# Decode attention inside a weight-bound stream: the key turns of a half batch moved behind three points of the half before it

## The chip, the cores and the metric

The kernel runs on one core of a Trainium2 chip. The metric is the time of one execution on the device in microseconds. A profile of one execution gives the trace. Engines are named as the profile names them: PE (TensorE, the matrix engine; PEld is its weight loads), DVE (VectorE), ACT (ScalarE), POOL (GpSimd), SP (SyncE, which issues DMAs).

## What is computed

One layer of a hybrid decoder for two groups of tokens with shared weights: a prompt of 512 tokens and a sample group of 8 sequences with 4 new tokens each, whose 4096 past positions lie in a paged cache. The layer is a gated feed-forward block, a mixer (a gated linear recurrence beside latent attention), and a second feed-forward block. The change is in the attention of the sample group over its cache, in the absorbed latent form:

```python
past_c = cache_kv_latent[l][page_table].reshape(Bs, past_len, KV_LORA)   # 256 wide
past_r = cache_k_rope[l][page_table].reshape(Bs, past_len, QK_ROPE)      # 64 wide
...
s = (einsum('bqhr,bsr->bhqs', ql, c_kv) + einsum('bqhd,bsd->bhqs', qr, k_rope)) * scale
s = where(k_pos <= q_pos, s, -inf)
p = softmax(s, axis=-1)
return einsum('bhqs,bsr->bqhr', p, c_kv)
```

Each of the 8 sequences has 16 queries (4 tokens by 4 heads) against 4096 keys.

## The kernel before

The prompt's tokens and the sample's are cut into two column halves, a and b (256 and 288 columns). Weights are fetched in tiles of 128x1024 (`wraw`, on SP's queue) and split into a high part on ACT (`wh`, L253) and a low part on DVE (`wl`, L254); every product takes three matmuls on PE (`wh` by high, `wh` by low, `wl` by high). Almost all of PE's time is this stream.

The decode of the sample group runs inside the second feed-forward block of column half a. Two generators are stepped in turn: `gb`, the feed-forward block (`ffn`), and `ga`, the decode (`decode`), so that the decode's small pieces stand among weight matmuls in program order. The order of each engine's instructions is then fixed when the program is built, by a scheduler that keeps to the program order as far as data allow. Each engine runs its list in order.

The feed-forward steps that are named below, all on column half a: `sil` from the gate's accumulator (DVE L337), three activations `sit` (ACT L323 to L325), the gate product (DVE L339), the product with the up projection (DVE L368), and the split of the result into `hha` (ACT L173) and `hla` (DVE L174). Down projections are copied or added into `ma` (ACT L393, DVE L395).

The decode goes by half batches, class `Half`: half n belongs to sequence n // 2 and holds 2048 of its keys (two gathered blocks `craw`, 128 partitions by 8 rows by 256). There are 16. A half passes these steps:

- `gather` and `gather_r` fetch the latent rows and the rotary rows (`rk`) by indirect DMA on POOL.
- `turn(st)`, four times: the keys of one group of 64 latent columns are turned by two 32x32-block transposes on DVE (`kh`, L1391), one for each block. Four `kh` buffers stand, so one half's turns fit.
- `score`: 64 small matmuls on PE against the four `kh`, in the order of the turns, and 16 against `rk` (L1409), one burst. Two copies bring the scores to `e` (L1411), and DVE takes the row maximum `mxh` (L1413; this instruction is kept as `top`).
- `peak`: PE transposes the maximum (`pm`, L1419), DVE reduces it (L1421) and spreads it with a mask, summed into `mbd` (L1424); ACT takes the exponential (L1425); DVE transposes the probabilities (`pt`, L1427); and 16 small copies place them in `pbuf` (L1431), 12 on ACT and 4 on DVE.
- `value`: 16 matmuls of `pbuf` with `craw` (L1440), the sequence's two halves into one accumulator; after the second half ACT copies it out (L1443) and `gathered` sums it on PE (L1448) and DVE (L1449).

`qsplit(b)` lays out the queries of sequence b in one of two buffers (L1261, two copies on DVE and two on ACT). In `score`, after `top` of a sequence's second half, it is called for the next sequence.

`decode` runs a step count n with five sub-steps, `st` 0 to 4. In step n the turns are those of half n - 2, whose score comes at `st` 4 (`RUN`); the half n - 3 has its `peak` at `st` 1 and its `value` at `st` 4, behind that score. `TURNS` says how many turns are written at each `st`: (2, 1, 1, 0, 0). The first one of a step is tied with `tc.issue_after` behind `top` of half n - 3: the scheduler may not place it earlier.

Of the kernel before, what the change touches and what calls it, by code (L numbers as in the profile page):

```python
# [14 lines left out]
ALU = mybir.AluOpType  # L15
# [6 lines left out]
NB = 8  # L22
# [22 lines left out]
SCALE = 1.0 / float(np.sqrt(192.0))  # L45
# [20 lines left out]
KHB = 4  # L66
STEPS = 5
PEAK, RUN = 1, 4
TURNS = (2, 1, 1, 0, 0)
LEVELS = (32, 16, 8, 4, 2, 1)  # L70
CH = 64

# [41 lines left out]
def hybrid_step_kernel(  # L114
# [5 lines left out]
    nc = tc.nc  # L120
# [12 lines left out]
    def mk(shape, dt, tag, bufs=1, pool=None):  # L133
        return (pool or cur[-1]).tile(shape, dt, name=tag, tag=tag, bufs=bufs)
# [10 lines left out]
    def ps(name, tag="ps", own=False):  # L145
        if tag == "ps" and not own:
            tag = CYC[turns[0] % 4]
            turns[0] += 1
        return pp.tile([P, 512], F32, name=name, tag=tag, bufs=NPS[tag])
# [422 lines left out]
    with scope("ffn0") as pool:  # L572
# [143 lines left out]
        if True:  # L716
            if True:
                sst.close()
                st = stg.enter_context(tc.tile_pool(name="st", bufs=1, side="right", reuse_waits="tile"))
# [73 lines left out]
    with scope("mix") as mx_:  # L793
# [293 lines left out]
        with scope("at2"):  # L1087
# [168 lines left out]
            def qsplit(b):  # L1256
                q = qbd[b % 2]
                bs = slice(b * 16, b * 16 + 16)
                for g in range(4):
                    gs = slice(g * 32, g * 32 + 32)  # L1260
                    (nc.scalar.copy if g % 2 else nc.vector.tensor_copy)(q[gs, :, g % 2 * 16 : g % 2 * 16 + 16], qrep[gs, :, bs])  # L1261
# [49 lines left out]
    with scope("dec"):  # L1311
# [3 lines left out]
        sel4, selL = dq[:, 0, 13 * P : 13 * P + 32], dq[:, 0, 13 * P + 32 : 13 * P + 48]  # L1315
# [45 lines left out]
        class Half:  # L1361
# [32 lines left out]
            def score(self):  # L1394
                q = qbd[self.b % 2]
                self.s = [ps("s", own=True) for _ in range(2)]
                for st, js in enumerate(JS):
                    for jj, j in enumerate(js):
                        for c in range(4):
                            for r in range(2):  # L1400
                                rs = slice(r * 64, r * 64 + 64)
                                as_ = slice(c % 2 * 4, c % 2 * 4 + 4)
                                if j < 8:
                                    kh = self.kh[st][rs, c // 2, as_, jj]
                                    out = self.s[r][c * 32 : c * 32 + 32, :P]
                                else:
                                    kh = self.rk[c // 2][rs, :, jj, as_].rearrange("p i a k -> p a i k")
                                    out = self.s[r][c * 32 : c * 32 + 32, :P].rearrange("p (a i k) -> p a i k", a=4, i=2)
                                nc.tensor.matmul(out, q[rs, j], kh, start=st + jj == 0, stop=st == len(JS) - 1 and jj == 1, skip_group_check=True)  # L1409
                for r in range(2):  # L1410
                    (nc.vector.tensor_copy if r else nc.scalar.copy)(self.e[:, r * P : r * P + P], self.s[r][:, :P])  # L1411
                self.mx = mk([P, 1], F32, "mxh", 2)
                self.top = nc.vector.tensor_reduce(self.mx, self.e, axis=AX.X, op=ALU.max)  # L1413
                if self.i and self.b + 1 < NB:
                    qsplit(self.b + 1)

            def peak(self):
                pm = ps("pm", "pm")[:, :P]
                nc.tensor.matmul(pm, self.mx.broadcast_to([P, P]), ident, start=True, stop=True, skip_group_check=True)  # L1419
                m = m3[:, self.i, self.bs]  # L1420
                nc.vector.tensor_reduce(m, pm.rearrange("p (g q) -> p q g", q=16), axis=AX.X, op=ALU.max)  # L1421
                mq = mk([P, 16], F32, "mq", 2)
                mb = mk([P, 1], F32, "mbd", 2)
                nc.vector.scalar_tensor_tensor(mq, m, -SCALE, selL, op0=ALU.mult, op1=ALU.mult, accum_out=mb)  # L1424
                nc.scalar.activation(self.e, self.e, AF.Exp, scale=SCALE, bias=mb, accum_out=Lc[:, self.i, 0, self.b : self.b + 1])  # L1425
                pt = mk([P, ROWS, 32], F32, "pt", 2)
                nc.vector.transpose(pt.rearrange("p a k -> p (a k)"), self.e)  # L1427
                for c in range(4):
                    for g in range(4):
                        src = pt[c * 32 : c * 32 + 32, g // 2 * 4 : g // 2 * 4 + 4, g % 2 * 16 : g % 2 * 16 + 16]  # L1430
                        (nc.scalar.copy if g else nc.vector.tensor_copy)(self.p[g * 32 : g * 32 + 32, c // 2, c % 2 * 4 : c % 2 * 4 + 4, self.i * 16 : self.i * 16 + 16], src)  # L1431

            def value(self, mate, c):
                i = self.i
# [16 lines left out]
        def decode():  # L1451
            H = [Half(n) for n in range(NH2)]
            blocks = [h_ for h_ in H for _ in range(2)]
            ups = [(h_, st) for h_ in H for st in range(len(JS) - 1)]

            def gather(n=1):
                for h_ in blocks[:n]:
                    h_.gather()
                del blocks[:n]

            def turn(top):
                if ups:
                    h_, st = ups.pop(0)
                    with tc.issue_after(top.ins) if top is not None else nullcontext():
                        h_.turn(st)

            for n in range(NH2 + 4):

                def at(k):
                    return H[n - k] if 0 <= n - k < NH2 else None  # L1470

                for st in range(STEPS):
                    if st == RUN and at(2):
                        at(2).score()
                    if n < 3 and st == 0:
                        gather(2 + n // 2)
                    if st == 0 and 0 <= n - 1 < NH2:
                        at(1).gather_r()
                    if st == PEAK and at(3):
                        at(3).peak()  # L1480
                    if st == 1 and at(4) and at(4).i:
                        at(4).gathered()
                    if st == RUN and at(3):
                        for c in range(2):
                            at(3).value(at(4), c)
                            gather()
                    if n > 1:
                        for i in range(TURNS[st]):
                            turn(at(3).top if at(3) and st + i == 0 else None)
                    yield  # L1490

        def decode_end():
# [33 lines left out]
            nc.vector.tensor_copy(oT[1][:, NH:, HS[1] - TS :], o[:, :P].rearrange("p (h t) -> p h t", h=NH))  # L1526

        ga, gn = decode(), decode_new()
        na, ib = STEPS * (NH2 + 2) + 4, 0
        for ia in range(na):  # L1530
# [191 lines left out]
```

## Time and profile before

| | |
|---|---|
| median of three runs | 1257.47 us (1255.41 to 1258.70) |
| the profiled execution | 1259.31 us |
| its span, first to last instruction | 1257.5 us |
| granted TensorE clock, mean | 0.994 |
| busy ACT / POOL | 59% / 8% |
| decode bursts (L1409), first and last start | 712.1 and 953.0 us |

The page gives busy time by engine, the span in slices, the chain of work that ended last and the costliest groups of instructions. A row of a timeline reads: start in us, duration in us, engine, line, operation, output <- inputs, shape, count, and in brackets the idle time of that engine before it and what ended it. In the list of waits a row gives who waited for what, the total in us, how often, and the longest. A window row gives the busy time of PE, PEld, DVE, ACT and POOL with their counts. A matmul on 32-bit floats stands as two records.

### The profile page before, as it was taken

What the parts mean: (1) busy time and instruction counts of PE and PEld (TensorE: products, weight loads), DVE (VectorE), ACT (ScalarE), POOL (GpSimd) and SP (SyncE); (2) the same over time, 40 slices, a digit from 0 to 9 for tenths busy, and PEclk for the clock granted to TensorE, in tenths of its full rate; (3) what the DMA queues carried; (4) which work ended last, traced back from release to release, by engine and by line L of the source; (5) the groups of instructions that cost most, each with busy time, mean ns of one, the idle gap of its engine ahead of it and who ended that gap; (6) DMA issues with size and microseconds to landing.
All of it is one profiled execution on the core that took longest, in us unless ns stands there. A gap on an engine that the chain in (4) does not pass through costs nothing.

```text
span 1257.5 us, 30075 instructions
## 1 busy us (share of the span) xinstructions
PE 1217.1 (97%) x12366; PEld 1155.1 (92%) x12366; DVE 965.2 (77%) x1945; ACT 739.1 (59%) x1559; POOL 105.2 (8%) x112
## 2 busy tenths in 40 slices
PE   8999999999999999999999999889999999999997
PEld 7999999999999988988888988778787999999997
DVE  7897778878679887877876988787887878466665
ACT  7675545454566654446668765554656777554454
POOL 0000000000000000000002243432530000000000
PEclk9999999999999999999999999999999999999999
DMA  6232323332165121324226769777786635545551
GB/s 235 85 118 94 99 95 101 101 98 84 51 226 166 60 91 58 104 79 145 82 86 242 278 220 322 257 254 279 251 270 218 207 106 191 191 135 182 151 152 59
DMA packets 73914, 195.63 MB, mean 156 GB/s; under 512 B 13136, under 2 KB 28528, under 8 KB 69040
## 3 DMA queue, kind: packets, MB, share of 16 engines
q1 hardware_dynamic: 64800, 150.50, 37.0%
q0 software_dynamic: 7680, 41.95, 9.3%
q8 instruction: 97, 1.59, 0.5%
q10 hardware_dynamic: 1296, 1.26, 0.4%
q14 instruction: 41, 0.34, 0.1%
HBM read 184.00 MB, written 9.67 MB: 154 GB/s over the span
## 4 chain that ended last, share of the span: by engine, by line
PE 85%; ACT 7%; DVE 5%; issue 2%; DMA 0%; SPq 0%; DVEq 0%; another core or an unknown queue 0%; ACTq 0%
PE acc L262 30%; PE acc L280 17%; PE dn L262 8%; PE Y L578 6%; PE X L578 4%; PE Z L578 4%; PE acc L734 3%; PE s L1409 2%; PE o L1440 2%; ACT wh L253 2%; DVE kh L1391 1%; ACT pbuf L1431 1%; PE pa L956 1%; PE s L1206 1%; DVE wl L254 1%
## 5 line engine op out<-in xcount | busy, mean ns | idle before, releaser
L253 ACT CAST wh<-wraw 128x1024 fp32r<-128x1024 f32 (+2 forms) x194 | 184.9, 958 | 180.7 <-PE acc L262 99.3
L254 DVE TENSOR_TENSOR wl<-wraw,wh 128x1024 fp32r<-128x1024 f32 (+2 forms) x194 | 214.8, 1110 | 81.6 <-ACT wh L253 75.7
L280 PE MATMUL acc<-uha,wh 128*128 128x256 f32 (+1 forms) x528 | 155.5, 295 | 0.7 <-issue 0.7
L280 PE MATMUL acc<-ula,wh 128*128 128x256 f32 (+1 forms) x528 | 151.8, 288 | 0.0
L280 PE MATMUL acc<-uha,wl 128*128 128x256 f32 (+1 forms) x528 | 151.3, 287 | 0.3 <-issue 0.2
L262 PE MATMUL acc<-uhb,wh 128*128 128x288 f32 (+1 forms) x432 | 128.0, 296 | 0.0
L262 PE MATMUL acc<-uhb,wl 128*128 128x288 f32 (+1 forms) x432 | 127.0, 295 | 1.0 <-DVE wl L254 0.7
L262 PE MATMUL acc<-ulb,wh 128*128 128x288 f32 (+1 forms) x432 | 127.5, 295 | 0.0
L280 PEld LDWEIGHTS acc<-uha,wh 128*128 128x128 f32 x528 | 100.5, 191 | 8.2 <-issue 7.6
L280 PEld LDWEIGHTS acc<-ula,wh 128*128 128x128 f32 x528 | 100.6, 191 | 1.5 <-issue 1.2
L280 PEld LDWEIGHTS acc<-uha,wl 128*128 128x128 f32 x528 | 100.5, 190 | 1.5 <-issue 0.9
L262 PEld LDWEIGHTS acc<-uhb,wl 128*128 128x128 f32 x432 | 81.2, 188 | 1.6 <-DVE wl L254 1.6
L262 PEld LDWEIGHTS acc<-uhb,wh 128*128 128x128 f32 x432 | 81.0, 187 | 0.2 <-ACT uhb L173 0.2
L262 PEld LDWEIGHTS acc<-ulb,wh 128*128 128x128 f32 x432 | 81.1, 188 | 0.1
L1383 POOL DMA_INDIRECT rk<-pool_r,idr x64 | 67.2, 1051 | 147.5 <-PE s L1409 124.5
L262 PE MATMUL dn<-hh,dh 128*128 128x272 f32 x256 | 74.3, 290 | 0.0
L262 PE MATMUL dn<-hh,dl 128*128 128x272 f32 x256 | 73.7, 288 | 0.0
L262 PE MATMUL dn<-hl,dh 128*128 128x272 f32 x256 | 73.6, 288 | 0.0
L280 PE MATMUL acc<-uhb,wh 128*128 128x272 f32 x176 | 52.8, 300 | 0.0
L262 PE MATMUL acc<-hlb,wh 128*128 128x288 f32 x176 | 52.1, 298 | 0.0
L262 PE MATMUL acc<-hhb,wh 128*128 128x288 f32 x176 | 51.8, 298 | 0.0
L262 PE MATMUL acc<-hhb,wl 128*128 128x288 f32 x176 | 51.4, 294 | 0.0
(634 smaller groups left out, 3875.7 us busy)
## 6 DMA issues: line engine op xcount, KB each, us to landing
wraw<-w_u SPq DMA_DIRECT2D x66, 512.0 KB
wraw<-w_g SPq DMA_DIRECT2D x65, 512.0 KB
wraw<-w_d SPq DMA_DIRECT2D x40, 384.0 KB
wraw<-w_in SPq DMA_DIRECT2D x24, 512.0 KB
wraw<-w_d SPq DMA_DIRECT2D x32, 320.0 KB
wraw<-w_d SPq DMA_DIRECT2D x16, 512.0 KB
wraw<-w_o SPq DMA_DIRECT2D x16, 512.0 KB
g_S<-state SPq DMA_DIRECT2D x4, 512.0 KB
```

The costliest lines, as they stand in the source:

```text
L253: nc.scalar.copy(wh[:, :kt], w[:, :kt])
L254: nc.vector.tensor_tensor(wl[:, :kt], w[:, :kt], f32(wh[:, :kt]), op=ALU.subtract)
L262: nc.tensor.matmul(out, a, b, start=n == 0, stop=n == last)
L280: nc.tensor.matmul(acc[:, :n], a[:, k], b[:, k], start=k + i == 0, stop=k == kt - 1 and i == 2)
L578: nc.tensor.matmul(bank, a[p][:, k], b[q][:, k], start=first and k + n == 0, stop=k == 3 and n == 2, skip_group_check=True)
L734: nc.tensor.matmul(accs[x, d], wts[d][p][:, k], hs[k // 2][q][:, k % 2, x], start=k + n == 0, stop=k == nf - 1 and n == 2)
L956: nc.tensor.matmul(po[es, c].rearrange("p (n m) -> p n m", m=m), kx[:, cs], up(qx[:, cs], m), start=True, stop=True, skip_group_check=True)
L1206: nc.tensor.matmul(s[:, :N], a_, b_, start=n == 0, stop=False, skip_group_check=True)
L1383: nc.gpsimd.indirect_dma_start(rk[:, i].rearrange("p j a k -> p (j a k)"), None, pool_r, off)
L1391: nc.vector.transpose(kh[:, g].rearrange("p a j k -> p a (j k)"), src)
L1409: nc.tensor.matmul(out, q[rs, j], kh, start=st + jj == 0, stop=st == len(JS) - 1 and jj == 1, skip_group_check=True)
L1440: nc.tensor.matmul(o[g : g + 32, :R], self.p[:, c, a], self.craw[c][:, a], start=i + c == 0 and a < 4, stop=i + c == 2 and a >= 4, skip_gr ...
```

## The change

```diff
-TURNS = (2, 1, 1, 0, 0)
+TURNS = (1, 1, 2, 0, 0)
...
                 self.top = nc.vector.tensor_reduce(self.mx, self.e, axis=AX.X, op=ALU.max)
-                if self.i and self.b + 1 < NB:
-                    qsplit(self.b + 1)
...
-                nc.vector.scalar_tensor_tensor(mq, m, -SCALE, selL, op0=ALU.mult, op1=ALU.mult, accum_out=mb)
+                self.spread = nc.vector.scalar_tensor_tensor(mq, m, -SCALE, selL, op0=ALU.mult, op1=ALU.mult, accum_out=mb)
...
-                        (nc.scalar.copy if g else nc.vector.tensor_copy)(self.p[g * 32 : g * 32 + 32, c // 2, c % 2 * 4 : c % 2 * 4 + 4, self.i * 16 : self.i * 16 + 16], src)
+                        put = (nc.scalar.copy if g else nc.vector.tensor_copy)(self.p[g * 32 : g * 32 + 32, c // 2, c % 2 * 4 : c % 2 * 4 + 4, self.i * 16 : self.i * 16 + 16], src)
+                        if g == 0:
+                            self.placed = put
...
+                    if st == 2 and at(2) and at(2).i and at(2).b + 1 < NB:
+                        qsplit(at(2).b + 1)
...
                     if n > 1:
-                        for i in range(TURNS[st]):
-                            turn(at(3).top if at(3) and st + i == 0 else None)
+                        for _ in range(TURNS[st]):
+                            turn(getattr(at(3), ("top", "spread", "placed")[st]) if at(3) else None)
```

Per step one turn is written behind `top` of the half before (the row maximum), one behind `spread` (the masked sum), and two behind `placed` (the last of DVE's four copies into `pbuf`), each tied there. Before, only the first of two turns at `st` 0 was tied, and the others had no tie. The call of `qsplit` moves from the end of `score` to `st` 2 of the step in which the sequence's second half is scored, which is ahead of that score. Nothing else changes; lines from the moved call on shift by two (L1421 becomes L1419, L1431 becomes L1429).

DVE's list from the maximum of half 0 (`mxh`) on, where half 1's turns stand (`kh` from `ha` and `hb`). Before:

```order
L1391 STREAM_TRANSPOSE kh<-hb 128x512
L1421 TENSOR_REDUCE q_8193<-pm 128x16
L337 TENSOR_TENSOR sil<-acc,rna 128x256
L1424 SCALAR_TENSOR_TENSOR mq,mbd<-q_8193 128x16
L1391 STREAM_TRANSPOSE kh<-ha 128x512
L1391 STREAM_TRANSPOSE kh<-hb 128x512
L1427 STREAM_TRANSPOSE pt<-q_8193 128x256
L254 TENSOR_TENSOR wl<-wraw,wh 128x1024
L1431 COPY pbuf<-pt 32x4x16 x4
L339 TENSOR_TENSOR sil<-sil,sit 128x256
L254 TENSOR_TENSOR wl<-wraw,wh 128x1024
L368 TENSOR_TENSOR sil<-sil,acc 128x256
```

The same place after the change, from the spread on:

```order
L1422 SCALAR_TENSOR_TENSOR mq,mbd<-q_8193 128x16
L1391 STREAM_TRANSPOSE kh<-ha 128x512
L1391 STREAM_TRANSPOSE kh<-hb 128x512
L1425 STREAM_TRANSPOSE pt<-q_8193 128x256
L254 TENSOR_TENSOR wl<-wraw,wh 128x1024
L1429 COPY pbuf<-pt 32x4x16 x4
L339 TENSOR_TENSOR sil<-sil,sit 128x256
L1391 STREAM_TRANSPOSE kh<-ha 128x512
L1391 STREAM_TRANSPOSE kh<-hb 128x512
L1391 STREAM_TRANSPOSE kh<-ha 128x512
L1391 STREAM_TRANSPOSE kh<-hb 128x512
L368 TENSOR_TENSOR sil<-sil,acc 128x256
```

The last two turns, four transposes, moved from ahead of the reduction of `pm` to behind the copies into `pbuf`.

DVE's list for half 11 (its keys are in `uhb` and `ha`), before, from the gate's `sil` on:

```order
L337 TENSOR_TENSOR sil<-acc,rna 128x256
L1391 STREAM_TRANSPOSE kh<-ha 128x512
L1391 STREAM_TRANSPOSE kh<-uhb 128x512
L1421 TENSOR_REDUCE q_8193<-pm 128x16
L1449 COPY q_8793<-o 128x4x16
L339 TENSOR_TENSOR sil<-sil,sit 128x256
L1424 SCALAR_TENSOR_TENSOR mq,mbd<-q_8193 128x16
L1391 STREAM_TRANSPOSE kh<-ha 128x512
L368 TENSOR_TENSOR sil<-sil,acc 128x256
L1427 STREAM_TRANSPOSE pt<-q_8193 128x256
L254 TENSOR_TENSOR wl<-wraw,wh 128x1024
L1431 COPY pbuf<-pt 32x4x16 x4
```

After, from the spread on:

```order
L1422 SCALAR_TENSOR_TENSOR mq,mbd<-q_8193 128x16
L1449 COPY q_8793<-o 128x4x16
L1391 STREAM_TRANSPOSE kh<-uhb 128x512
L1425 STREAM_TRANSPOSE pt<-q_8193 128x256
L1391 STREAM_TRANSPOSE kh<-ha 128x512
L1429 COPY pbuf<-pt 32x4x16 x4
L368 TENSOR_TENSOR sil<-sil,acc 128x256
L1391 STREAM_TRANSPOSE kh<-uhb 128x512
L1391 STREAM_TRANSPOSE kh<-ha 128x512
L1391 STREAM_TRANSPOSE kh<-uhb 128x512
L174 TENSOR_TENSOR hla<-sil,hha 128x256
L1391 STREAM_TRANSPOSE kh<-ha 128x512
```

Ahead of the gate's `sil` stood five of the half's transposes before, and stand two after; six now follow the spread, four of them the copies, and `hla` stands before the last one. In halves 2, 5 and 8 the end of the list reads the same way. ACT's list at half 11 is unchanged (exponential, `wh`, twelve copies to `pbuf`, `hha`); at half 2 it is not:

```order
-L1425 ACTIVATE q_8193<-q_8193,mbd 128x256
-L253 CAST wh<-wraw 128x768
-L173 CAST hha<-sil 128x256
-L1431 COPY pbuf<-pt 32x4x16 x12
+L1423 ACTIVATE q_8193<-q_8193,mbd 128x256
+L253 CAST wh<-wraw 128x768
+L1429 COPY pbuf<-pt 32x4x16 x12
+L173 CAST hha<-sil 128x256
```

There `hha`, for which `hla` waits, moved behind the twelve copies. The copies of `qsplit` (L1261) keep their places on both engines. PE's list is the same but for the first burst, whose pieces between weight matmuls are fewer. SP's and POOL's lists are the same.

## The prediction

> **What bounds the kernel now.** I read the page first: the span, the busy shares, the chain that ended last.
>
> ```profile
> span 1257.5 us, 30075 instructions
> ...
> PE 1217.1 (97%) x12366; PEld 1155.1 (92%) x12366; DVE 965.2 (77%) x1945; ACT 739.1 (59%) x1559; POOL 105.2 (8%) x112
> ...
> PE 85%; ACT 7%; DVE 5%; issue 2%; DMA 0%; SPq 0%; DVEq 0%; another core or an unknown queue 0%; ACTq 0%
> ```
>
> TensorE is the bound. Its order of work is the same before and after, but for pieces of the first burst, so the change can only alter what TensorE waits for. Two more views narrow this to the stretch in which half batches 1 to 15 are decoded (half h is batch h//2, part h%2): the busy time by window, and TensorE's waits from 700 to 970.
>
> ```profile
> 728.00:970.00 242.00, 222.35 (x4116) 194.98 (x4115) 192.44 (x434) 141.15 (x383) 85.92 (x85) 0.99 0.76 257
> ...
> PE o L1440 <- issue: 7.9, 5, 2.5
> PE s L1409 <- issue: 4.0, 2, 2.0
> ...
> PE o L1440 <- ACT sit L323: 1.0, 1, 1.0
> ...
> PE o L1440 <- ACT pbuf L1431: 0.9, 1, 0.9
> PE pm L1419 <- DVE mxh L1413: 0.6, 1, 0.6
> ```
>
> TensorE (the first pair) idles 242.0 - 222.35 = 19.7 us there: the most that any edit of the decode order can win. Only the last two waits, 1.5 us, are of the chain that the change shortens. The 11.9 us of "issue" sit in or just behind a score burst, and I read them as code loads: TensorE's instructions arriving late. One is this, in half 8's burst:
>
> ```profile
> 841.84 2.03 PE L1409 MATMUL s<-kh,q 64*32 64x128 f32 x128
> ...
> 846.34 0.41 PE L1409 MATMUL s<-rk,q 64*32 64x128 f32 x3 [2.00 <-issue]
> ...
> q8 instruction: 1, 0.02, 1.0%
> ...
> q8 instruction: 97, 1.59, 0.5%
> ```
>
> The window 841 to 847 holds one packet of the instruction queue (third row). The page has 97 for 2 x 12366 TensorE instructions, 255 each. A burst issues 320 records in 2.5 us, so one packet covers less than a burst. VectorE is 192.44/242 = 80% busy, with little room to catch up.
>
> **The layout of the next batch's queries** (four copies at L1261, ahead of seven batches) is written two steps earlier, but its copies stand in the same places in both built programs, on VectorE and ScalarE. I cost it at 0.
>
> **The turns.** Count and kind are unchanged: eight transposes a half. Two leave for the wait behind `spread`, four go behind `placed`. Before, most of them filled VectorE's gap right after `top`. What they must meet is the burst: it reads turn by turn, and the last transpose is needed after 52 of its 64 key matmuls. Half 11's 128 key records take 892.23 to 894.00, 1.77 us, so that point is start + 1.77 x 52/64 = 1.44 us.
>
> Half 1 can be read off almost directly:
>
> ```profile
> 732.72 1.05 ACT L253 CAST wh<-wraw 128x1024 fp32r<-128x1024 f32 x1 [2.68 <-PE pm L1419]
> ...
> 733.99 0.50 ACT L1425 ACTIVATE q<-q,mbd 128x256 f32<-128x256 f32 x1
> ...
> 734.06 0.67 DVE L1391 STREAM_TRANSPOSE kh<-hb 128x512 f32<-128x512 f32 x1
> 734.65 0.41 DVE L1427 STREAM_TRANSPOSE pt<-q 128x256 f32<-128x256 f32 x1
> 734.98 1.18 DVE L254 TENSOR_TENSOR wl<-wraw,wh 128x1024 fp32r<-128x1024 f32 x1
> 736.09 0.82 DVE L1431 COPY pbuf<-pt 32x64 f32<-32x64 f32 x4
> 736.94 0.42 DVE L339 TENSOR_TENSOR sil<-sil,sit 128x256 f32<-128x256 f32 x1
> ...
> 735.73 2.03 PE L1409 MATMUL s<-kh,q 64*32 64x128 f32 x128
> ```
>
> `pt`, the low weight part, the four copies and the gate product keep their order, and `pt` can't go earlier, since ScalarE's exponential before it (L1425) stands behind a weight cast that starts at 732.72 either way. Behind the gate product now stand four transposes: 737.30 + 4 x 0.61 = 739.75 (the step of two neighbours is 0.59 to 0.63, as 734.06 to 734.65). Needed: 735.73 + 1.44 = 737.17. **Late by 2.55**, where before the last was done at 734.73.
>
> Half 11 adds a second stop:
>
> ```profile
> 884.62 0.42 DVE L1413 TENSOR_REDUCE mxh<-q 128x1 f32<-128x256 f32 x1 [0.46 <-DVE q L1411]
> 884.95 0.70 DVE L1391 STREAM_TRANSPOSE kh<-uhb 128x512 f32<-128x512 f32 x1
> ...
> 888.16 0.42 DVE L337 TENSOR_TENSOR sil<-acc,rna 128x256 f32<-128x256 f32 x1
> ...
> 890.99 0.71 DVE L1391 STREAM_TRANSPOSE kh<-ha 128x512 f32<-128x512 f32 x1
> ...
> 888.16 1.05 ACT L253 CAST wh<-wraw 128x1024 fp32r<-128x1024 f32 x1 [2.53 <-PE acc L280]
> ...
> 891.62 1.04 ACT L253 CAST wh<-wraw 128x1024 fp32r<-128x1024 f32 x1
> 892.68 3.08 ACT L1431 COPY pbuf<-pt 32x64 f32<-32x64 f32 x12
> 895.78 0.41 ACT L173 CAST hha<-sil 128x256 fp32r<-128x256 f32 x1
> ...
> 892.23 2.03 PE L1409 MATMUL s<-kh,q 64*32 64x128 f32 x128
> 894.00 0.74 PE L1409 MATMUL s<-rk,q 64*32 64x128 f32 x32
> ```
>
> After the two transposes of the first turn VectorE now stands before the gate's read (L337), which needs TensorE until 888.16; the other six of the eight transposes, which ran between 886.17 and 891.70 (first and last row above), are no longer in front of `spread`. Then, at the spacing of the rows of before: low part 889.21 to 890.31 (behind the cast), maximum, gate product, spread to 890.95, output copy and one transpose to 891.77, `pt` 891.9, one transpose, four copies to 893.7, `sil` to 894.03, three transposes to 895.84. Now comes `hla` (L174), which needs ScalarE's `hha`, queued behind the twelve `pbuf` copies: 896.15. So `hla` at 896.17, the last transpose 896.53 to 897.2. Needed: 893.67. **Late by 3.5.**
>
> The same laying out for the others (start of burst, last transpose of after, late):
>
> | half | burst | last | late | | half | burst | last | late |
> |---|---|---|---|---|---|---|---|---|
> | 1 | 735.73 | 739.75 | 2.55 | | 8 | 841.84 | 844.9 | 1.6 |
> | 2 | 747.71 | 752.4 | 3.25 | | 10 | 878.25 | 881.3 | 1.6 |
> | 3 | 764.01 | 766.65 | 1.2 | | 11 | 892.23 | 897.2 | 3.5 |
> | 4 | 780.64 | 782.65 | 0.55 | | 12 | 904.99 | 908.6 | 2.15 |
> | 5 | 797.31 | 801.0 | 2.25 | | 14 | 935.62 | 938.05 | 0.95 |
> | 6 | 811.19 | 814.85 | 2.2 | | 15 | 950.83 | 952.55 | 0.25 |
> | 7 | 826.21 | 828.1 | 0.45 | | 9, 13 | | | 0 |
>
> Halves 2, 5, 8 and 11 have the `hla` stop. The sum is **22.5 us**. TensorE's queue stands while it waits: weight matmuls, value products and `pm` behind the burst all move by as much, and ScalarE and VectorE, which wait for them, move along.
>
> **What the lateness lies over.** In halves 4 to 8 and 13 to 15 a code load already holds TensorE (the seven "issue" waits of L1440 and L1409 and the 1.0 us that is put down to `sit`). A wait inside the burst lets that load come in meanwhile, so of the two only the longer counts: in halves 4 to 8, 14 and 15 the shorter ones are 0.55 + 1.6 + 1.0 + 0.45 + 1.6 + 0.95 + 0.25 = 6.4 us, which cost nothing. The ends are 0, if a load starts only after the wait, and this 6.4. I take 6.4, since the packet of half 8 moves while TensorE stands.
>
> [...]
>
> **What goes.** The values behind half 12's burst waited 0.9 us for `pbuf`; with TensorE later that goes. The `pm` wait of 0.6 goes, since the burst ahead of it is late while VectorE runs on. Together 1.5 (ends 0 and 1.5).
>
> **Where code blocks end.** TensorE's built program has 177 instructions that only wait, where there were 229, so each block ends later in the work, by 49 instructions at half 15. The loads behind these two bursts would then be needed only among or behind the value products, where there is more time:
>
> ```profile
> 925.79 0.62 PE L1440 MATMUL o<-mb,pbuf 128*32 128x256 f32 x2 [0.72 <-issue]
> ...
> 955.34 0.85 PE L1440 MATMUL o<-ulb,pbuf 128*32 128x256 f32 x12 [1.98 <-issue]
> ```
>
> I take 2 off, between 2.7 off (both gone) and 2 on (a load that now meets half 9's burst and costs what half 8's did).
>
> Sum: 22.5 - 6.4 - 1.5 - 2 = **+12.6 us**. The span is 1257.5, the profiled execution took 1259.3, the median of the three runs is 1257.5; so the execution would be 1271.9, and the median 1257.5 + 12.6 = **1270.1**.
>
> **Rivals.**
> - *Covered or made up (within 0.3%).* Some stops in my layout are shorter than written, since VectorE has idle time in the stretch, most of it before `wl` (the row is below). Half the lateness, 11.25, and the same credits leave +1.3: 1259. Against it: the four copies and four transposes behind `pt` are 0.8 + 2.4 us in every half, and `pt` ends less than 3.2 us before the burst in half 1. Chance 0.15.
> - *The shorter chain wins.* If every last transpose meets start + 1.44, only the credits stay: 1257.5 - 1.5 - 2.7 = 1253.3. The point from which it decides is a last transpose within 1.44 us of the burst's start. For it: in half 1 of before it was ready a microsecond ahead. Against: half 1 laid out above. Chance 0.08.
> - *Code loads cover nothing.* Then 22.5 - 1.5 = +21: 1278.5. Against it: the idle 2.00 us with a packet in its window. Chance 0.15. [...]
> - *The edit does not do what it says*: true for the query copies, not for the turns, whose rows move. Its time is 1257.5, inside the first rival.
>
> ```profile
> L254 DVE TENSOR_TENSOR wl<-wraw,wh 128x1024 fp32r<-128x1024 f32 (+2 forms) x55 | 59.3, 1081 | 19.4 <-ACT wh L253 13.9 <-ACT ma L393 2.8 <-issue 2.3
> ```
>
> **Numbers.** My case, 1264 to 1276, has 0.62. Slower takes that and the third rival. A measurement of this kernel can tell about 0.3% from no change, 3.8 us. Faster 0.08, same 0.15, slower 0.77. The range from 1257 to 1278 leaves out the second rival and what lies over the third.
>
> **What would show it.** In the profile after: a wait "PE s L1409 <- DVE kh L1391" of some 15 to 22 us over a dozen places, longest in halves 2 and 11, where "hla" waits for ACT; the "issue" waits down from 11.9 to about 5; `pbuf` and `mxh` gone from TensorE's list. Wrong it is if the bursts find their turns ready (no such wait), or if the issue waits stay as they are under the lateness.

## The result, and the profile after

Measured: **1248.37 us** (1246.72 to 1249.47, six runs) against 1256.44 (1253.43 to 1258.95, six runs) of the kernel before beside them; the ratio is 0.9935, 95% interval 0.9916 to 0.9954. The change is faster by 8 us, where 12.6 us slower was forecast. The profiled execution of after took 1246.72 us.

The page of after (span, busy time, chain):

```profile
span 1244.9 us, 30022 instructions
...
PE 1211.4 (97%) x12366; PEld 1150.8 (92%) x12366; DVE 964.6 (77%) x1945; ACT 739.2 (59%) x1559; POOL 109.0 (9%) x112
...
PE 85%; ACT 6%; DVE 5%; issue 2%; DMA 1%; SPq 0%; DVEq 0%; ACTq 0%
```

TensorE's waits in after from 700 to 970 (who waited for what, total us, times, longest), and its busy time while it decodes:

```profile
PE s L1409 <- DVE kh L1391: 5.2, 7, 1.2
PE o L1440 <- issue: 5.0, 6, 1.3
PE o L1448 <- ACT q L1443: 0.9, 1, 0.9
PE acc L280 <- DVE wl L254: 0.4, 1, 0.4
PE s L1409 <- issue: 0.2, 1, 0.2
```

```profile
728.00:960.00 232.00, 220.44 (x4134) 194.60 (x4133) 194.26 (x442) 142.89 (x385) 88.75 (x84) 1.00 0.78 273
```

The bursts do wait for their turns, as forecast, but for 5.2 us in seven rows and not for 15 to 22. The issue waits fell from 11.9 to 5.2 us, `pbuf` and `mxh` are gone. While it decodes TensorE idles 232.0 - 220.4 = 11.6 us, where it idled 19.7 (16.9 in before_alone, a later profile of the kernel before, from 728 to 970).

**Two conditions.** To read the numbers below: each profile fell into one of two conditions, whatever the kernel, and the profile of before that the forecast rests on was taken in the worse one. In the *clean* condition the trace holds some 1530 records of the semaphores of POOL's gathers between 675 and 975 us, and of TensorE's signals (the semaphore updates that the trace names as what ends the other engines' waits for a matmul) in the decode none comes over 0.1 us behind the end of the matmul that gives it (at most 0.07 in after); before takes 1256 to 1258 us beside these. In the *held-back* condition 40 to 50% of those records are missing, 41 to 70 of some 250 signals come 0.7 to 4 us late, and issue waits of 0.3 to 1 us turn up among weight matmuls, most of them 430 to 515 instructions behind a burst's start; before takes 1263 to 1266 us beside them. Two chips showed both. After's profile above is clean, and its six times lie within 3 us. The first profile of before (851 records, 41 late signals) is held back, though the six times of before that stand beside after's (1253.43 to 1258.95) are as in clean sets. One execution of each set is kept as a trace, and beside held-back ones single times of before go down to 1252.86 us, so that not every execution of such a set need be held back.

One of the six executions of after_again took 2345 us; it lies far from all others, its cause is not known, and the ratio leaves it out.

| run | condition | median us | ratio to before beside it (95%) |
|---|---|---|---|
| after, as above | clean | 1248.37 | 0.9935 (0.9916 to 0.9954) |
| after_third (after) | clean | 1247.48 | 0.9924 (0.9905 to 0.9942) |
| before_alone (before) | clean | 1256.81 | 1.0003 (0.9984 to 1.0022) |
| before_shift_alone | clean | 1248.65 | 0.9936 (0.9915 to 0.9957) |
| after_shift_alone | clean | 1255.79 | 0.9992 (0.9975 to 1.0009) |
| turns_2_1_1_last | clean | 1244.55 | 0.9922 (0.9894 to 0.9950) |
| copies_only | held back | 1262.06 | 0.9992 (0.9962 to 1.0023) |
| before_again (before) | held back | 1262.61 | 0.9986 (0.9962 to 1.0011) |
| before_shift | held back | 1267.72 | 1.0024 (0.9997 to 1.0050) |
| after_shift | held back | 1289.32 | 1.0207 (1.0170 to 1.0245) |
| after_again (after) | held back | 1291.97 | 1.0220 (1.0164 to 1.0275) |
| after_fourth (after) | held back | 1291.60 | 1.0228 (1.0186 to 1.0271) |
| counts_only | held back | 1268.31 | 1.0034 (1.0000 to 1.0068) |
| spread_only | held back | 1275.09 | 1.0088 (1.0055 to 1.0121) |
| turns_2_1_1, five times | held back | 1262.2 to 1265.7 | 0.9981 to 1.0008 |

### The profile page after: what moved, and what is told of

Its sections match the earlier page's. It is cut to its first block, busy times and chain, and to the rows that moved or that the text cites. A ratio compares the mean times of both kernels' runs of the same rounds, so it can differ in the third digit from the quotient of the medians.

```text
span 1244.9 us, 30022 instructions
## 1 busy us (share of the span) xinstructions
PE 1211.4 (97%) x12366; PEld 1150.8 (92%) x12366; DVE 964.6 (77%) x1945; ACT 739.2 (59%) x1559; POOL 109.0 (9%) x112
## 4 chain that ended last, share of the span: by engine, by line
PE 85%; ACT 6%; DVE 5%; issue 2%; DMA 1%; SPq 0%; DVEq 0%; ACTq 0%
PE acc L262 30%; PE acc L280 16%; PE dn L262 8%; PE Y L578 7%; PE X L578 4%; PE Z L578 4%; PE acc L734 3%; PE s L1409 2%; PE o L1440 2%; ACT wh L253 2%; ACT pbuf L1429 1%; PE pa L956 1%; PE acc L291 1%; DVE kh L1391 1%; PE s L1206 1%
```

## Experiments on the condition

**copies_only**: the layout of the queries moved, turns as before.

```diff
-                if self.i and self.b + 1 < NB:
-                    qsplit(self.b + 1)
...
+                    if st == 2 and at(2) and at(2).i and at(2).b + 1 < NB:
+                        qsplit(at(2).b + 1)
```

> The layout of the next queries moved alone, turns as before. All theories: the same rows on every engine as before, so the time of before, 1256.4 us within 0.3%. What this second profile of before's work is to tell: in the first one TensorE's signals came up to 3.8 us behind the matmul that gives them, some 40 times between 690 and 980 us, and never after the change. Theory 'kernel' (the signals are late because of before's order): late again, and TensorE idle about 19.7 us between 728 and 970. Theory 'one execution' (that profiled run, the slowest of six, was disturbed): no signal over 0.1 us late, idle about 15 to 16, with the waits at a code block's end (0.6 to 2.8 us each, ten of them, 15 in sum) unchanged.

No difference in time from before, both in the held-back condition. The signals are late again (45 of 248), so this is no accident of one execution.

**after_again, after_third, after_fourth** are after, **before_again and before_alone** are before, without an edit.

> The changed kernel once more, beside before, on the chip of these runs. Of six profiles so far five show TensorE's signals late (40 to 65 of 250 between 690 and 980 us by more than 0.7 us) and 'issue' waits of 0.3 to 1.0 us among the weight matmuls 430 to 500 instructions behind a burst's start; the one without is that of after. Theory C (an executing state: TensorE's signals and issue back up behind its dense bursts, whatever the order, and after's profile was taken where they don't): late again here, and the gain of 8 us shrinks or turns, since late signals hold VectorE's gate read and so the turns behind it: a ratio between 1.00 and 1.02, with waits for kh of 10 us and more. Theory D (the changed order itself keeps the signals on time): no late signals, no such issue waits, ratio 0.993.

Theory C held against D in this set: 58 late signals, and a ratio of 1.022, just above C's range.

> The changed kernel a third time beside before, to separate the kernel from the condition it runs in. In the first profile of after the trace holds all records of semaphores in the decode (1531 of the DMAs between 675 and 975 us) and no signal of TensorE is late; in the second one, of the same program 43 us slower, 40 to 65 per cent of them are missing and 58 signals are late. Theory C (condition): either both come together again (records missing, signals late, 1285 to 1296 us, ratio 1.02) or neither (all records, no late signal, 1247 to 1250); then the ratio to before on that chip tells what the change does without the back-up: 0.993 by the verdict shown, near 1.000 if before was held back by the condition then. A mixed picture (records missing and 1248 us, or all records and 1290) would refute C.

Neither late nor missing: 1247.48, and a ratio of 0.9924, as in the first runs.

> The kernel before, unchanged, profiled on the same chip as the changed one below. Theory C (condition of the chip): with all semaphore records there (1531 of the DMAs between 675 and 975 us) and no late signal, its profile shows what before costs without the back-up, 1250 to 1256, and the change is worth 2 to 8 us; where the chip holds back, records are missing and it takes 1256 to 1275. Theory D (the order): even on a chip where after keeps all records and takes 1248, before loses records, signals up to 3 us late, 1253 to 1260.

Held back, 1262.61 us, so this set doesn't tell what before costs in the clean condition.

> The changed kernel as the marker of the chip's condition: 1246 to 1251 with all semaphore records, or 1285 to 1296 with 40 per cent or more missing; nothing between.

Held back too, on the chip on which after_third was clean; of all times of after none lies between 1252 and 1287. So the two conditions came together with the kernel and the chip unchanged.

> The kernel before, unchanged, as the only kernel beside the reference runs of itself, which is how both runs of after at 1247 to 1248 us were taken; the three runs of after at 1290 us had two or three other kernels beside them, on the same chip in one case, so the condition goes with the company and not with the chip. Theory D (alone, the order decides: before backs up, after doesn't): records of the DMAs' semaphores missing (some 850 of 1531), 40 or more late signals, 1254 to 1259 us. Theory C (the company alone decides): all records, no late signal, and 1250 to 1256 us from the waits at block ends (15 us) alone.

Clean: 1531 records and no late signal, so theory C; only its range was too low by 1 us. D is out: the order of after isn't what keeps the signals on time. Nor is it the company of other kernels, as some of the expectations have it: turns_2_1_1 was held back three times with nothing but before beside it. What decides the condition stays open.

TensorE's waits in before_alone from 700 to 970 are before without the disturbance:

```profile
PE o L1440 <- issue: 9.1, 5, 2.5
PE s L1409 <- issue: 4.3, 2, 2.8
PE o L1440 <- ACT q L1411: 0.9, 1, 0.9
PE o L1448 <- ACT q L1443: 0.9, 1, 0.9
PE o L1440 <- ACT pbuf L1431: 0.9, 1, 0.9
```

The wait for `mxh` of the first profile isn't there, nor are issue waits among weight matmuls: what is left stands, but for the fourth and fifth row, at the ends of TensorE's blocks of 256 instructions, 16.0 us in all (the gaps between starts there, less the usual step; the third row is the block end of half 6, put down to another releaser).

## Experiments on the block ends

The instructions ahead of which TensorE stands still for its code have, counted from the program's start (weight loads and waiting instructions included), the numbers 193, 449, 705 and so on, in every trace. That these waits are code loads shows in the DMA records of the six clean profiles: wherever TensorE stands still for over 0.7 us at such an end in the decode, one packet of 16384 bytes of the instruction queue went out 0.5 to 3.6 us behind the block end ahead, and TensorE goes on 2.2 to 2.8 us behind that packet. For halves 1 to 15 of these profiles, the place of the first block end from 36 instructions ahead of a burst's start on, counted from that start, against the wait at the next one, 256 instructions later:

| first end at | halves | wait us, mean | least to most |
|---|---|---|---|
| 36 before to 1 before | 14 | 0.1 | 0 to 1.1 |
| 0 to 49 | 5 | 1.0 | 0 to 2.2 |
| 50 to 79 | 10 | 2.0 | 0.7 to 2.9 |
| 80 to 109 | 10 | 1.5 | 0 to 2.5 |
| 110 to 139 | 19 | 1.1 | 0 to 2.8 |
| 140 to 216 | 32 | 0.04 | 0 to 0.6 |

A burst has 320 instructions in 2.5 us, the values behind it 64 more. An end at 50 to 139 puts the next at 306 to 395, when nearly all of the block ran at the burst's pace; a later end lies where the block runs on into slower work (in after, weight matmuls start 0.12 us apart). To move the ends and nothing else, small matmuls with an unused result go under TensorE's first wait of 5.2 us (for `xq`): **before_shift** and **before_shift_alone** are before with 41 and 46 of them, **after_shift** and **after_shift_alone** after with 16 and 13.

```diff
-            pr = ps("pr", PRT)
+            pr = ps("pr", PRT); [nc.tensor.matmul(pr[:TS, :32], ones[:, :TS], ones[:, :32], start=True, stop=True, skip_group_check=True) for _ in range(46 if x == 0 else 0)]
```

> Before, with 41 small matmuls (164 instructions, result unused) ahead of TensorE's first work, under its first wait of 5.2 us; nothing else moves. The end of every block of 256 TensorE instructions then stands 164 instructions earlier in the work. Positions of the block end that falls into or next to the burst, from burst start, halves 1 to 15: 89, 85, 13, -49, 195, 192, 156, 153, 81, 17, 5, 2, -34, 195, 159, where before had -4, -8, 176, 114, 102, 99, 63, 60, -12, 180, 168, 165, 129, 102, 66. Theory A (a block whose predecessor's end falls 30 to 130 instructions into the burst comes late): 15.1 us of these waits fall to 4 to 5 (halves 1, 2, 9), time 1246 us, as much as the whole change gave. Theory B (the gain came from VectorE's order alone): 1256, or 1 to 3 more for the added matmuls.

> After, with 16 such matmuls (64 instructions) in front. Block ends in halves 1 to 15 at 189, 187, 119, 60, 52, 52, 20, 20, -48, 148, 140, 140, 108, 84, 52; after had -4, -6, 182, 123, 115, 115, 83, 83, 15, -45, -53, -53, 171, 147, 115. Theory A: the waits at block ends grow from 7.2 to about 12 us, so 1248.4 + 5 = 1253; before_shift is then the faster of the two. Theory B: 1248, and 8 below before_shift.

Both were held back. The waits at block ends fell in before_shift (16.4 in copies_only, 11.5 here), but the others among TensorE's gaps grew as much (12.2 to 18.5): what it doesn't wait at a block end it waits a little later. Theory A failed there; after_shift is as slow as after itself in that condition.

> Alone beside before (the clean condition: all records, no late signals). Before, with 46 small matmuls (184 instructions, result unused) under TensorE's first wait. Block ends from burst start, halves 0 to 15: -54, 69, 65, -7, 187, 175, 172, 136, 133, 61, -3, -15, -18, -54, 175, 139. Theory A (block ends in a burst): an end at 60 to 70 costs about 2, at 130 to 140 about 0.5, the others 0, so 7 to 8 us of waits where before alone had 16.0, and with fewer waits over 1.5 us fewer stretches of half clock behind them (1 or 2 for 4): 1246 to 1250. Theory B (the order on VectorE is the gain): 1257, as before.

**The shift alone gives a gain as large as that of the change**: 1248.65, ratio 0.9936. The waits at block ends are 10.0 us (three over 1.5 us, where before_alone had six), in these rows of 700 to 970:

```profile
PE s L1409 <- issue: 3.0, 2, 2.1
PE o L1440 <- issue: 2.3, 1, 2.3
PE o L1440 <- DVE sil L339: 1.8, 1, 1.8
```

The third is the block end of half 2, put down to another releaser.

> Alone beside before. After, with 13 small matmuls (52 instructions) in front, as many as its program has fewer than before: block ends from burst start, halves 0 to 15: 78, -55, -57, 131, 72, 64, 64, 32, 32, -36, 160, 152, 152, 120, 96, 64, near the places that before has (129, -4, -8, 176, 114, 102, 99, 63, 60, -12, 180, 168, 165, 129, 102, 66). Theory A: waits at block ends 12 to 15 us instead of after's 6 to 7, clock halvings again, and the 7 us of late turns stay: 1254 to 1260, ratio 0.998 to 1.003, so the gain is gone. Theory B: 1248, ratio 0.993.

**And the shift back takes it away**: 1255.79, ratio 0.9992. The same rows of this run:

```profile
PE s L1409 <- issue: 7.1, 5, 2.1
PE s L1409 <- DVE kh L1391: 5.2, 7, 1.3
PE o L1440 <- issue: 4.2, 2, 2.4
```

Block ends cost 15.0 us instead of 6.2 to 6.9, the wait for `kh` is unchanged. Theory A is shown from both sides, in the clean condition.

**What a long wait brings with it.** Windows of before_alone (length, then PE busy; the third number from the end is the granted clock):

```profile
785.40:788.50 3.10, 0.58 (x12) 0.35 (x9) 3.00 (x7) 0.00 (x0) 2.48 (x3) 1.00 0.80 291
788.50:791.90 3.40, 3.40 (x19) 3.05 (x15) 1.47 (x4) 0.62 (x2) 2.55 (x3) 0.50 0.85 246
843.30:846.50 3.20, 0.42 (x9) 0.18 (x9) 1.38 (x2) 1.69 (x5) 1.90 (x2) 1.00 0.88 268
846.50:849.90 3.40, 3.40 (x33) 1.40 (x32) 3.24 (x7) 0.19 (x1) 2.50 (x3) 0.50 0.69 239
```

Two block ends leave TensorE idle for 2.5 and 2.8 us, and the next 3.4 us run at half the clock. before_alone has four such stretches up to 980 (one of 10.2 us), after_shift_alone four, both profiles of clean after none. In the clean profiles each stretch inside the decode follows 1.8 to 2.9 us of idle time in the 6 us ahead of it; idles of 1.3 us and less have none. Not every long idle has one, and the 1.7 us at 689 before the decode has it in some runs only, so this is read from the traces and not shown by an experiment.

## Experiments on the order of the turns

**counts_only**: the new counts with the old tie. **spread_only**: one turn behind the maximum, three behind the masked sum. **turns_2_1_1**: the ties of the change with the counts of before, so that the last turn alone stands behind the placed probabilities.

```diff
-TURNS = (1, 1, 2, 0, 0)
+TURNS = (2, 1, 1, 0, 0)
```

> The counts 1, 1, 2 in place of 2, 1, 1 and the moved copies, but the old tie: only the first turn of a step is held behind the maximum. VectorE's rows stand as before in nearly all places, TensorE waits at 229 places as before, block ends as before. If the ties are the change: the ratio to before is 1.000 within 0.003. If the written place alone did it, 0.993.

1.0034 (1.0000 to 1.0068), held back. In that condition after itself shows no gain but a loss of 2.2%, so what this run shows is that the counts alone don't bring that loss (turns_2_1_1, below, shows it of the ties alone). That the gain is gone with the old tie follows only from theory A, since this program has the 229 waiting instructions of before; no clean run shows it.

> One turn behind the maximum and three behind the masked sum, none behind the placed probabilities. Block ends as in after to one instruction, but for halves 3 and 9. Theory B1 (lateness costs): the transposes no longer stand behind the placed probabilities, the waits of the scores for kh fall below 2 us and the time falls 3 to 5 us below after_again. Theory E (VectorE's order around the gate read decides): the gate read now stands behind all transposes in most halves, 1.2 to 2.4 us later, so the down product's input comes later and the time rises by 5 to 15 us over after_again.

Slower than before by 0.9%, faster by 1.3% than after_again in the same set; the waits for `kh` are 6.3 us in 17 rows, where after_again has 14.9. So in the held-back condition the rise of theory E did not come; B1 has the direction, but neither of its sizes (waits below 2 us, 3 to 5 us faster) fits the 6.3 us and the 17 us. No run shows it in the clean condition.

> The change with the old counts: two turns behind the maximum, one behind the masked sum, one behind the placed probabilities. TensorE's rows and block ends are those of after, so theory A alone gives 1248.4. Theory B has two parts. B1, lateness: with two transposes instead of four behind the placed probabilities the waits of the scores for the turns, 5.2 us in six rows after, fall below 2, so 1244 to 1245. B2, relief: what was won is that VectorE stands freer between the maximum and the masked sum; with two more transposes there a part of it is lost, so 1249 to 1251.

> Ties of the change with the old counts 2, 1, 1, once more. On a chip where after takes 1248: theory B1 (lateness of the last two turns costs 5 us there) 1243 to 1245; theory B2 (freeing VectorE behind the maximum is the gain) 1249 to 1253. On a chip where after takes 1290: 1264 as before.

> Alone beside before. The change's ties with the old counts: two turns behind the maximum, one behind the masked sum, only one behind the placed probabilities. 177 waiting instructions and the block ends of after to the instruction, so the waits at block ends stay at 6 to 7 us. This sizes the lateness term (5.2 us of waits of the scores for kh in after, 7 with resumption, all but 1 of it in halves 2, 5, 8 and 11). If the wait comes from the two transposes behind ScalarE's late hha only: it stays in half 2 and 8, falls in 5 and 11, and the time is 1245 to 1247. If the four transposes behind the placed probabilities are it: kh falls under 1, and 1241 to 1243. If the two more transposes between the maximum and the masked sum cost what they save: 1248 to 1250.

> The same kernel once more, since the run before it was one with late signals and missing records (before 1264.9 beside it). Should this run be clean (before 1256 to 1258, all records): waits at block ends 6 to 7 us as in after. If only halves 2 and 8 keep their wait for kh (the transposes behind ScalarE's late hha): 1245 to 1247. If kh falls under 1 us: 1241 to 1243. If the two more transposes behind the maximum cost what they save: 1248 to 1250. Should it again be one with late signals: 1262 to 1266, ratio 1.00.

> As for the two runs of this kernel before it, which both had late signals and came out at 1262 to 1263 us, ratio 0.998. Clean (before 1256 to 1258, all records): 1245 to 1247 if only halves 2 and 8 keep their wait for kh, 1241 to 1243 if that wait falls under 1 us, 1248 to 1250 if the two more transposes behind the maximum cost what they save. With late signals: 1262 to 1266.

> As for the three runs before. Clean (before 1256 to 1258 beside it, all records): 1245 to 1247 if halves 2 and 8 keep their wait for kh, 1241 to 1243 if that wait falls under 1 us, 1248 to 1250 if the two more transposes behind the maximum cost what they save. With late signals (before 1263 to 1266): 1262 to 1266, ratio 1.00.

Five sets held back, all at the time of before; the waits for `kh` are 3 to 6 us in these where after has 15 and 16. The last set is clean: **1244.55 us, ratio 0.9922**. Its waits:

```profile
PE o L1440 <- issue: 7.5, 6, 2.3
PE o L1448 <- ACT q L1443: 0.9, 1, 0.9
PE s L1409 <- DVE kh L1391: 0.2, 1, 0.2
```

The 5.2 us for `kh` are gone, by two transposes less behind the placed probabilities (B1). The time is still not the 1241 to 1243 that was expected for that case, since the waits at block ends did not stay as in after: the row of issue waits is 7.5 us where after has 5.0 in as many places, although the block ends stand at the same instructions. Of the difference 1.5 us stand in halves 5 and 8, where in after the wait for `kh` stands ahead of the load, and 1.1 us in half 4, where it has no such wait; the same place costs more in one profile than in another. By its median this version is 3 to 4 us below after in the clean condition, where the intervals overlap, and it is some 2% faster than after in the other one.

## Why the prediction was wrong, step by step

**The account.** Step by step along TensorE's order, from before_alone to after_third (both clean), 690 to 980 us: waits at block ends -10.1, waits for `kh` +7.0 (with the restart of the burst), `pbuf` -1.9, small issue gaps behind the block ends and pace of the matmuls at the clock granted -8.1 together, nearly all of it in stretches at half the clock, others +0.5; sum -12.6 us of these two profiles, of which the medians show 8 to 10. Some 3 us of this sum are not the change's: they lie ahead of 725 us, where before_alone runs 10.2 us at half the clock and after_third doesn't, but turns_2_1_1_last, clean and fastest of all, does (the first row is before_alone, the second turns_2_1_1_last):

```profile
693.00:703.20 10.20, 9.52 (x45) 8.99 (x44) 8.31 (x16) 5.92 (x16) 2.74 (x3) 0.50 0.65 229
...
693.00:703.20 10.20, 9.53 (x45) 8.99 (x44) 8.20 (x16) 5.93 (x15) 2.88 (x3) 0.50 0.65 214
```

**The term that failed by size: where code blocks end.** Forecast -2 (between -2.7 and +2); measured -10.1, and with the half clock from 725 us on some -15. The mechanism was the forecast one, and it was placed right: 52 fewer waiting instructions move the ends, 49 at half 15. But the step counted only two loads that leave the burst, of halves 13 and 15. It overlooked that of half 14 (2.2 us in before_alone, none in after), and it let those of halves 4 to 8 stand, although their ends move too, by 9 to 23 instructions, on the slope of the table above. These cost 11 us in before_alone, 9 in turns_2_1_1_last and 5 to 7 in after, where the lateness took a share. It took the price of a load from its idle time alone; the half clock behind it wasn't in the sum at all. "The most that any edit of the decode order can win" was given as the idle 19.7 us, and pace is beyond that.

**The other term that failed by size is the lateness: forecast 22.5, measured 7.0 in the clean condition.** The waits are real, but late signals of the first profile were laid out as if they were stops of the program. In half 1 the step that failed is "ScalarE's exponential ... stands behind a weight cast that starts at 732.72 either way". In the first profile of before TensorE's maximum and VectorE's read of it stand so:

```profile
731.15 0.38 PE L1419 MATMUL pm<-ident,mxh 128*128 128x128 f32 x2
...
732.80 0.29 DVE L1421 TENSOR_REDUCE q<-pm 128x16 f32<-128x128 f32 x1 [0.46 <-PE pm L1419]
```

VectorE was free and started 1.3 us behind the matmul's end; the cast of 732.72 starts 1.57 us behind this matmul's start. In before_alone, and then in after:

```profile
733.70 0.38 PE L1419 MATMUL pm<-ident,mxh 128*128 128x128 f32 x2
733.78 1.05 ACT L253 CAST wh<-wraw 128x1024 fp32r<-128x1024 f32 x1 [1.22 <-PE acc L280]
```

```profile
730.37 0.38 PE L1417 MATMUL pm<-ident,mxh 128*128 128x128 f32 x2
730.45 1.05 ACT L253 CAST wh<-wraw 128x1024 fp32r<-128x1024 f32 x1 [1.03 <-PE acc L280]
```

In both it starts 0.08 us behind. The 1.5 us were a late signal, not a stop of the kernel's order, and the forecast for half 1 (2.55) is too high by about that: measured 0.9. In half 11 the step is "the gate's read (L337), which needs TensorE until 888.16". The gate's last matmul in the first profile, then the same matmul and the read in after:

```profile
883.96 0.28 PE L280 MATMUL acc<-uha,wl 128*128 128x256 f32 x1
```

```profile
877.99 0.28 PE L280 MATMUL acc<-uha,wl 128*128 128x256 f32 x1
...
878.30 0.42 DVE L337 TENSOR_TENSOR sil<-acc,rna 128x256 f32<-128x256 f32 x1 [0.69 <-PE acc L280]
```

In the first profile that matmul ends at 884.24 and its signal stands in the trace at 888.13, 3.9 us late; in after the read starts 0.03 us behind the matmul's end. Measured against its burst's start the read comes 2.2 us earlier than it was laid, and half 11 came out at 1.4 us, for 3.5. Halves 2, 5 and 8 came out at 1.4 to 1.5 each (forecast 3.25, 2.25 and 1.6), 14 at 0.4. So the stops at `hla` were seen rightly, but sized too high in halves 2, 5 and 11. The rest came out at 0, where 8.4 us were forecast. Late signals are not the reason in all of them: in half 12 (forecast 2.15) the reduction of `pm` starts 0.3 us ahead of the burst in before_alone too, behind seven of the half's transposes, and 4.0 us ahead in after, behind two. As I read these rows, taking the turns away from in front of it freed more than the layout allowed for.

**In the held-back condition the forecast of the lateness holds.** Waits of after_fourth from 700 to 990:

```profile
PE s L1409 <- DVE kh L1391: 16.1, 35, 1.4
PE acc L280 <- issue: 7.0, 14, 0.8
PE acc L262 <- issue: 1.5, 3, 0.7
```

16.1 us in 35 rows (forecast 15 to 22 over a dozen places), 25.5 along TensorE's order against before_again. I read it from the two orders: late signals hold VectorE's reads of the gate and of the maximum, and in after six transposes stand behind these, where in before most stood ahead. The time, 1292 us, lies above the whole forecast range. So the forecast sized the lateness of the condition that the first profile was taken in; clean runs of the kernel don't have it.

**Lateness over code loads: -6.4, of which about 1 us came in the clean runs.** Only halves 5 and 8 have both a late turn and a load there. Half 8 of after, then of turns_2_1_1_last, whose block ends stand at the same places and whose turn is not late:

```profile
837.19 1.75 PE L1409 MATMUL s<-kh,q 64*32 64x128 f32 x104
840.18 0.53 PE L1409 MATMUL s<-kh,q 64*32 64x128 f32 x20 [1.24 <-DVE kh L1391]
...
843.31 0.42 PE L1440 MATMUL o<-ulb,pbuf 128*32 128x256 f32 x4 [1.28 <-issue]
```

```profile
838.13 2.03 PE L1409 MATMUL s<-kh,q 64*32 64x128 f32 x128
...
843.68 0.42 PE L1440 MATMUL o<-ulb,pbuf 128*32 128x256 f32 x4 [2.28 <-issue]
```

From the burst's start to the matmul behind the load it is 6.1 us with the wait of 1.24 us and 5.6 us without it; in half 5 it is 5.6 us with a wait of 1.10 and 4.7 without. So 0.7 and 0.2 us of the lateness are covered, by one profile of each. The time of such a load differs from profile to profile by as much, so these sizes are rough. In the held-back condition the waits are longer and the cover is whole, as in half 8 of after_fourth, with the instruction queue's row for the window 860.91 to 862.31:

```profile
862.31 0.42 PE L1409 MATMUL s<-kh,q 64*32 64x128 f32 x8 [1.40 <-DVE kh L1391]
...
866.22 1.07 PE L1440 MATMUL o<-ulb,pbuf 128*32 128x256 f32 x16
...
q8 instruction: 1, 0.02, 4.3%
```

The packet goes out while TensorE waits for its turn, and the values then run without a stop. So a load can come in under the lateness, as was forecast; it failed in size, because the clean lateness is short and in half 8 of after the packet goes out only at 840.98, behind the wait. What sets the time of the packet stays open. In the table above the wait is next to nothing behind ends at 140 and later (0.04 us on average) and small behind those just ahead of a burst (0.1 us), but not behind ends up to 139 instructions into it (averages of 1.0 to 2.0 us).

**Right**: the query copies cost nothing (0.9992, in the held-back condition). `pbuf` went (-1.9 with resumption), though not because TensorE is late, as was forecast: turns_2_1_1_last has next to no lateness and no such row either. The 0.6 us for `mxh` was a late signal and is absent in before_alone too. The issue waits at 5.2 hit "about 5" by luck: mainly the ends' places brought them there, and not the cover that was forecast.

**The rivals.** None names block ends as the gain. "The shorter chain wins" was nearest in time (1253.3) and is not what happened: the waits of that chain are 1.5 us.

## What to carry to other kernels

Ahead of a forecast, see whether the profile is itself disturbed: releases that come a microsecond or more behind the end of what releases them (1.3 us in half 1 of the first profile, 3.9 in half 11) were no stops of the program here, and a layout built on them inherits them. Where one engine bounds the kernel and runs bursts of short instructions, the count of its instructions ahead of a burst is a variable of its own (46 small matmuls took before to 0.9936 of its time, and 13 took after from 0.9935 back to 0.9992); shift it with dummies under an early wait, on the kernel before as well, ahead of crediting an edit's order. An order that leaves work behind two reads has to be timed with slow releases too: after gains 0.7% clean and loses 2.2% held back, while one turn moved back keeps the gain and loses nothing.

## What was not expected of the hardware

TensorE's signals came up to 4 us late all through the decode (3.9 us in half 11 of the first profile of before), while the same program on another occasion showed none over 0.1 us late; with it went missing records of semaphores (851 for 1531) and a loss of 7 us for before and 43 us for after. Whether the recording causes the delay or suffers from the same cause can't be told from these runs. A block end in a burst cost up to 2.9 us of idle time, and behind some of these TensorE ran 3.4 us at half the clock, as behind the 2.5 and 2.8 us of before_alone.
